# A two-layer encoder trunk on one core: the order of layer two's beginning left to the scheduler, and one operand sum moved from VectorE to an accumulating transfer

## The chip, the core and the metric

The kernel runs on one core of one Trainium2 chip. The metric is the device time of one execution in microseconds (us), as the median of several runs. The profile is one further execution, taken by the hardware profiler. Its engines are PE (TensorE; PEld is its weight load), DVE (VectorE), ACT (ScalarE), POOL (GpSimd) and SP (SyncE, which here only issues transfers). Each engine works through its own queue in order; engines wait for each other through semaphores.

## The reference

Two layers, each on the residual stream x of 512 rows by 2048 columns, all in float32:

```python
for l in range(DEPTH):                      # DEPTH = 2
    h = rmsnorm(x, pre_norm_g[l])
    z = h @ w_in[l]                         # 2048 -> 4928 columns
    q_lat, kv_lat, k_pe, gb, gc, xin, q_mem, gate = split_cols(z)
    ...                                     # latent attention, 8 heads: a_out
    c_out = short_gated_conv(gb, gc, xin, conv_w[l])
    mem_n = rmsnorm(mem, mem_norm_g[l])     # 256 memory tokens
    m_out = memory_attention(q_mem, mem_n, w_mk[l], w_mv[l])   # keys = mem_n @ w_mk, values = mem_n @ w_mv
    y = jnp.concatenate([a_out, c_out, m_out], axis=-1) * jax.nn.silu(gate)
    o = y @ w_o[l]                          # 2048 -> 2048
    x = x + rmsnorm(o, post_norm_g[l])
```

## The kernel before, in words

**Products in three matmuls.** Every float32 operand is split into a high piece (a rounded copy, made by ACT) and a low piece (operand minus high piece, made by DVE). A product is three matmuls: high by high, high by low, low by high (lines 296 to 298). For streamed weights the high piece is `wh` and the low piece `wl`: lines 212 and 216 for plain weights, lines 226 and 227 for the memory weights, which also take a gain. Three `wh` and three `wl` buffers rotate, so ACT can prepare a high piece once the matmuls three weight tiles back have ended.

**Seven block products.** The large products are cut into 2 by 2 blocks and done with seven block products P1 to P7 (a Strassen-Winograd scheme) whose operands are sums of blocks. Each block product runs over four steps c = 0 to 3; a step of 512 columns is 12 matmuls. The right-hand sums live in four raw tiles `T`, one for each c: T starts as block B11, becomes T1 for P5, T2 for P6 and T4 for P4. Sums are formed in two ways. `more` is a transfer on POOL's queue that adds a weight block into the tile as it arrives; it is issued once the low piece of the previous use is made. `plus` loads the block into a raw tile of its own, and DVE adds it (line 200); `other` adds a tile that is there already (line 202). Eight raw tiles rotate.

**The output projection** (`out_proj`) works on two pairs of 512-column blocks. The second pair uses the plan `FOUR`: passes P2, P1, then P3, P5, P6 and P7 interleaved by c, then P4. In it, `P5` adds block (0, 1), loaded by `plus`, to T and keeps the loaded tile under the name B12; `P6` adds the B22 tile to T; `P7` adds the kept B12 to B22.

**Side work.** What follows a block product (squares of the result for the post-norm, line 1205; the gain, line 1210; the residual sums `part`, line 1249) is put in a queue of deferred pieces. After each step the step's room is added to a budget (at most 2.5), and pieces are taken off while the budget covers their cost: 0.7 for a square and gain, 1.2 for half a residual row block.

**Layer two's beginning** comes right behind layer one's P4: 16 steps of memory keys and values (`mk` and `mv`, eight each, 24 and 12 matmuls), between them the transposes of the normalised rows, row block t = 0 to 3 in four banks each (call them T0 to T15; line 639 on PE). The normalisation of row block t is a Square over 2048 elements on ACT (`row_factor`, line 620), a power on POOL, and a scaled copy on ACT (`next_rows`, line 1277); the Square waits for both residual halves of that block. Then the input projection's first group starts with P1.

**What sets the order.** PE, SP and POOL always issue in the order in which the program was written. For DVE and ACT a scheduler chooses, except in written regions (`in_order(True)` to `in_order(False)`), where their instructions keep the written order among themselves. The scheduler still decides where instructions from outside a written region fall among those inside. In layer one the region runs from P1 of the last column pair, through layer two's memory steps and transposes, to the end of P1 and P2 of layer two's first group. In layer two it covers the last column pair alone.

Of the kernel before, what the change touches and what calls it, by code (L numbers as in the profile page):

```python
# [251 lines left out]
def encoder(tc, x, mem, positions, pre_norm_g, w_in, q_norm_g, w_uq, kv_norm_g, w_ukv, conv_w,  # L252
# [3 lines left out]
    nc = tc.nc  # L256
    depth = w_in.shape[0]
# [15 lines left out]
    add = pr.add  # L273
# [198 lines left out]
    def group(left, key, w, block, slot, passes, final, hold=None, by_two=False):  # L472
# [9 lines left out]
        def unit(q, c):  # L482
            def of(name, *loads, more=None, plus=None, alloc=None, **kw):
                return Unit((key, name, c), [block(h, j, c) for h, j in loads],
                            None if more is None else block(*more, c), None if plus is None else block(*plus, c), alloc,
                            **kw)
            if passes is FOUR and q in ("P5", "P6", "P7"):
                return {"P5": lambda: of("T", plus=(0, 1), keep=(key, "B12", c)),
                        "P6": lambda: of("T", other=(key, "B22", c)),
                        "P7": lambda: of("B22", other=(key, "B12", c))}[q]()  # L490
            if q == "P1":
                return of("P1" if apart else "T", (0, 0))
            if q == "P5":
                if passes is FIRST:
                    return of("T", (0, 0), more=(0, 1))
                return of("T", *([(0, 0)] if apart else []), plus=(0, 1))
            return {"P6": lambda: of("T", more=(1, 1)), "P4": lambda: of("T", more=(1, 0), alloc=hold),
                    "P2": lambda: of("P2", (1, 0)), "P3": lambda: of("B22", (1, 1)),
                    "P7": lambda: of("B22", plus=(0, 1))}[q]()
# [767 lines left out]
    def next_factor(t):  # L1267
        def f():
            pr.until(lambda: f"xo{t}" in G)
            xt, og = G[f"xo{t}"]  # L1270
            G[f"xr{t}"] = row_factor(xt, og)
        return f

    def next_rows(t):
        def f():
            xt, og = G.pop(f"xo{t}")
            nc.scalar.activation(og, xt, AF.Copy, scale=G[f"xr{t}"])
            G[f"hs{t}"] = og
        return f
# [52 lines left out]
    for l in range(depth):  # L1332
        G["left"] = L = Left(True)
        C, gs, owns = projection(l)

        def use(L=L):
            G["left"] = L
            G["ys"] = {}
        turn = [lambda l=l, t=t: transpose_rows(l, t, G[f"hs{t}"]) for t in range(NT)]
        if l == 0:  # L1340
            add(use)
            def turn_half(t, h, on=None):
                return lambda: transpose_rows(0, t, G[f"hs{t}"], (2 * h, 2 * h + 1), on)
            add(turn_half(0, 0))
            add(lambda: first_rows(1, (0,)))
            add(pr.begin_prep(1))
            add(lambda: left_half(0, (0,)))
            add(pr.begin_prep(2))
            add(turn_half(1, 0, nc.scalar))
            add(lambda: first_rows(1, (1,)))  # L1350
            add(lambda: left_half(1, (0,)))
            add(pr.begin_prep(3))
            add(lambda: first_factor(2))
            add(turn_half(0, 1))
        else:
            ms = mem_steps(l)
            put(ms[:1])
            for i in range(2):
                add(lambda i=i: mem_reload(2 + i))
            add(next_factor(0))  # L1360
            put(ms[1:2])
            add(next_rows(0))
            put(ms[2:3])
            add(use)
            side = {0: next_factor(1), 1: next_rows(1), 3: next_factor(2), 5: next_rows(2), 7: next_factor(3),
                    9: next_rows(3)}
            ms = [(f, u, 0.3 if k < 11 else 1.0) for k, (f, u, _) in enumerate(ms)]
            for n in range(16):
                t, q = n // 4, n % 4
                add(lambda t=t, q=q: transpose_rows(l, t, G[f"hs{t}"], (q,), nc.vector))  # L1370
                if t < 2 and q % 2:
                    add(lambda t=t, q=q: left_half(t, (q // 2,)))
                if t >= 2 and q == 3:
                    add(lambda t=t: right_half(t - 2))
                put(ms[n + 3:n + 4])
                if n in side:
                    add(side[n])
        (a, b), (a1, b1) = gs[0][:2], gs[1][:2]
        add(owns[0])
        if l == 0:  # L1380
            put(a[:1])
            add(first.close)
            add(turn_half(1, 1))
            add(lambda: left_half(0, (1,)))
            add(lambda: left_half(1, (1,)))
            add(lambda: first_rows(2))
            add(lambda: first_factor(3))
            add(lambda: first_rows(3))
            put(a[1:], b[:1])
            add(turn[2])  # L1390
            add(lambda: right_half(0))
            put(b[1:3])
            add(turn[3])
            add(lambda: right_half(1))
            put(b[3:])
        else:
            put(a, b)
            add(in_order(False))
        add(owns[1])
        put(a1, b1)  # L1400
        put(*gs[0][2:], *gs[1][2:])
        add(owns[2])
        put(gs[2][0])
        conv = [(conv_turn(l, c, C), []) for c in range(4)]
        put(weave(gs[2][1] + gs[2][2], conv, 2), *gs[2][3:])
        add(owns[3])
        put(*gs[3])
        add(owns[4])
        if l == 0:
            add(positions_load)  # L1410
        g4 = [s for steps in gs[4] for s in steps]
        put(g4[:4])
        add(lambda l=l, C=C: latents_begin(l, C))
        put(g4[4:8])
        if l > 0:
            add(lambda C=C: k_rope(C))
        put(g4[8:16])
        if l == 0:
            add(mem_load)
            G["mTd"] = dram.tile([4, P, D], F32, name="mTd")  # L1420
        lat = [latent_turn(l, "cq", j) for j in range(4)] + [latent_turn(l, "ckv", j) for j in range(2)] + [k_rope_turn] * (l > 0)
        gm = lambda t, C=C: C["gm"][:, t, :]
        more = [(f, []) for f in [gate_turn(12 + j, gm, j) for j in range(4)] + [qm_turn(j, C) for j in range(4)] + lat]
        if l == 0:
            more.insert(8, (mem_rows, []))
        put(weave(g4[16:], more[:11], 1))
        put(more[11:])
        gates = [gate_turn(j, lambda t, C=C, j=j: C["ga0" if j < 4 else "ga1"][:, t, :], j % 4) for j in range(8)]
        G["left"] = Y = Left(False)
        g0, g1, gains, fetch = out_proj(l)  # L1430

        def low(p):
            return lambda: G["left"].split("A12", p, G["ys"][2 + p][:, :, :256])

        def use_y(Y=Y):
            G["left"] = Y

        def sums(p):
            def f():
                a, b = G["ys"][p], G["ys"][2 + p]  # L1440
                left = G["left"]
                pr.defer(1.2, lambda: left.split("A11", p, a[:, :, :256]))
                pr.defer(1.2, lambda: left.split("A22", p, b[:, :, 256:]))
                combine(left, p, a[:, :, :256], b[:, :, :256], a[:, :, 256:], b[:, :, 256:])
            return f

        last_pair = {0: [(sums(0), []), g0[0][0]], 1: [g0[0][1]], 2: [g0[0][2]], 3: [g0[0][3]],
                     4: [g1[0][0]], 5: [g1[0][1]], 6: [g1[0][2]], 7: [g1[0][3]]}

        def route(l=l):  # L1450
            if l == depth - 1:
                G["src"], G["dst"] = G["dst"], out[0]
            else:
                G["src"], G["dst"] = x[0], dram.tile([S, D], F32, name="xs")
        add(route)
        mixer(l, C, gates, {6: [(use_y, []), (low(0), [])], 7: [(low(1), [])]}, last_pair)
        add(sums(1))
        add(gains(0))
        put(*g0[1:])
        add(gains(1))  # L1460
        four = {q: [g1[2][4 * c + k][1][0] for c in range(4)] for k, q in enumerate(("B22", "B12"))}
        for t, u in enumerate((g1[1][3][1][0], four["B22"][0], four["B22"][1], four["B12"][1])):
            u.behind = fetch(t)
        add(in_order(True))
        put(g1[1], g1[2][:14])
        if l + 1 < depth:
            for i in range(2):
                add(lambda i=i: mem_reload(i))
        put(g1[2][14:], g1[3])
        if l + 1 == depth:  # L1470
            add(pr.settle)
            add(in_order(False))
# [27 lines left out]
```

## Time and profile before

| | |
|---|---|
| runs, median of 3 | 1535.54 us (1534.11 to 1536.19) |
| the profiled execution, its own time | 1535.69 us |
| its span in the trace | 1533.9 us |
| mean granted TensorE clock | 0.994 |
| PE busy | 1494.0 us, 97% of the span |
| DVE busy | 1171.2 us |
| ACT busy | 861.9 us |

The span is what the trace covers; the profiled time lies 1.79 us above it. In a timeline row the first number is the start in us from the span's start, the second the duration; `[2.07 <-ACT wh L226]` at its end says how long the engine had been idle and what ended that. `x2` merges two instructions. In a row of stretches (windows) each engine has its busy time and its number of instructions; behind them stand the granted clock, the DMA engines' busy share and GB/s.

### The profile page before, as it was taken

How to read it: one execution, taken by the hardware profiler on the slowest of the kernel's cores; microseconds unless marked ns; L12 is line 12 of the kernel's file. 1: busy time of each engine (PE TensorE's matmuls, PEld its weight loads, DVE VectorE, ACT ScalarE, POOL GpSimd, SP SyncE). 2: the span in 40 equal slices, each digit the busy share in tenths (PEclk: the TensorE clock that was granted, in tenths of full speed). 3: DMA queues.
4: the chain of work that ended last, by engine and by line, in shares of the span. 5: the costliest groups of instructions: out<-in, count | busy, mean ns of one | idle time of the engine just before them, and what ended most of it. 6: DMA issues, size and time to landing. Idle time of an engine off the chain costs nothing.

```text
span 1533.9 us, 20277 instructions
## 1 busy us (share of the span) xinstructions
PE 1494.0 (97%) x7613; PEld 1278.0 (83%) x7613; DVE 1171.2 (76%) x1518; ACT 861.9 (56%) x1307; POOL 171.9 (11%) x189
## 2 busy tenths in 40 slices
PE   8999999999999999999998999999999999999995
PEld 7788888987898888888787888888988888888884
DVE  5987877675887668888778977887676776689787
ACT  8643534454667768645476543534454686775543
POOL 0212020221000000110210012020211000003001
PEclk9999999999999999999999999999999999999998
DMA  8989685979473112495776899695978421037743
GB/s 310 222 209 236 178 191 156 209 193 249 137 231 126 42 42 67 113 228 197 221 273 220 224 240 229 180 196 152 206 201 199 160 69 42 29 104 153 266 123 123
DMA packets 142030, 266.42 MB, mean 174 GB/s; under 512 B 17032, under 2 KB 39660, under 8 KB 138604
## 3 DMA queue, kind: packets, MB, share of 16 engines
q1 hardware_dynamic: 108904, 191.15, 38.8%
q0 software_dynamic: 32896, 73.93, 24.8%
q8 instruction: 59, 0.97, 0.3%
q14 instruction: 39, 0.32, 0.1%
q10 hardware_dynamic: 132, 0.05, 0.0%
HBM read 250.42 MB, written 14.68 MB: 173 GB/s over the span
## 4 chain that ended last, share of the span: by engine, by line
PE 76%; DVE 9%; ACT 6%; issue 6%; DMA 3%; POOL 1%; DVEq 0%; POOLq 0%; ACTq 0%; SPq 0%
PE P L297 18%; PE P L298 18%; PE P L296 18%; DMA wr<-in_w_in_dram 3%; DVE wl L216 2%; PE ptp L1064 2%; ACT wh L212 2%; PE tps L824 1%; PE o L297 1%; PE sc L296 1%; PE sc L297 1%; PE sc L298 1%; PE o L298 1%; PE o L296 1%; PE sc L1044 1%
## 5 line engine op out<-in xcount | busy, mean ns | idle before, releaser
L212 ACT CAST wh<-wr 128x1024 fp32r<-128x1024 f32 (+1 forms) x404 | 416.2, 1033 | 469.2 <-PE P L298 272.0
L216 DVE TENSOR_TENSOR wl<-wr,wh 128x1024 fp32r<-128x1024 f32 (+1 forms) x404 | 481.2, 1195 | 211.3 <-ACT wh L212 209.7
L296 PE MATMUL P<-wh,S 128*128 128x512 f32 (+1 forms) x896 | 346.7, 387 | 0.0
L297 PE MATMUL P<-wl,S 128*128 128x512 f32 (+1 forms) x896 | 345.1, 385 | 1.5 <-DVE wl L216 1.3
L298 PE MATMUL P<-wh,S 128*128 128x512 f32 (+1 forms) x896 | 344.1, 384 | 0.4 <-DVE S L434 0.4
L297 PE MATMUL P<-wl,A 128*128 128x512 f32 (+1 forms) x656 | 252.6, 385 | 7.1 <-DVE wl L216 7.1
L296 PE MATMUL P<-wh,A 128*128 128x512 f32 (+1 forms) x656 | 253.3, 386 | 0.5 <-ACT wh L212 0.5
L298 PE MATMUL P<-wh,A 128*128 128x512 f32 (+1 forms) x656 | 251.6, 384 | 0.5 <-DVE A L434 0.5
L297 PEld LDWEIGHTS P<-wl,S 128*128 128x128 f32 x896 | 168.6, 188 | 32.8 <-DVE wl L216 3.4
L298 PEld LDWEIGHTS P<-wh,S 128*128 128x128 f32 x896 | 168.6, 188 | 31.4 <-DVE S L434 0.9
L296 PEld LDWEIGHTS P<-wh,S 128*128 128x128 f32 x896 | 168.5, 188 | 29.7
L142 POOL DMA_DIRECT2D wr<-in_w_in_dram x84 | 101.7, 1211 | 555.3 <-DVE wl L216 400.1
L297 PEld LDWEIGHTS P<-wl,A 128*128 128x128 f32 x656 | 123.2, 188 | 30.9 <-DVE wl L216 9.4
L296 PEld LDWEIGHTS P<-wh,A 128*128 128x128 f32 x656 | 123.1, 188 | 23.4 <-ACT wh L212 1.6
L298 PEld LDWEIGHTS P<-wh,A 128*128 128x128 f32 x656 | 123.1, 188 | 23.2 <-DVE A L434 1.2
L200 DVE TENSOR_TENSOR wr<-wr,wr 128x1024 f32<-128x1024 f32 (+1 forms) x100 | 118.7, 1191 | 8.7 <-DMA wr<-in_w_in_dram 6.7
L1050 ACT ACTIVATE P<-sc,nm 128x512 f32<-128x512 f32 (+1 forms) x96 | 59.9, 625 | 36.7 <-DVE nm L1047 35.9
L1047 DVE TENSOR_REDUCE nm<-sc 128x1 f32<-128x512 f32 (+1 forms) x96 | 57.0, 596 | 12.2 <-PE sc L1045 6.7
L1053 ACT ACTIVATE P<-P,rec 128x512 f32<-128x512 f32 (+1 forms) x96 | 61.6, 658 | 6.0 <-DVE rec L1052 6.0
L302 DVE TENSOR_TENSOR PT<-ptp,PT 128x512 fp32r<-128x512 f32 (+1 forms) x96 | 56.2, 594 | 8.8 <-ACT PT L301 8.6
L226 ACT ACTIVATE wh<-wr,cols 128x512 fp32r<-128x512 f32 x64 | 43.6, 717 | 22.7 <-PE P L298 7.0
L227 DVE SCALAR_TENSOR_TENSOR wl<-wr,cols,wh 128x512 fp32r<-128x512 f32 x64 | 45.8, 747 | 13.4 <-ACT wh L226 13.4
(270 smaller groups left out, 2226.6 us busy)
## 6 DMA issues: line engine op xcount, KB each, us to landing
wr<-in_w_in_dram SPq DMA_DIRECT2D x172, 512.0 KB, 4.4
wr<-in_w_o_dram SPq DMA_DIRECT2D x72, 512.0 KB, 4.0
wr<-in_w_in_dram POOLq DMA_DIRECT2D x68, 512.0 KB, 7.1
wr<-in_w_in_dram SPq DMA_DIRECT2D x40, 416.0 KB, 3.8
wr<-in_w_o_dram POOLq DMA_DIRECT2D x24, 512.0 KB, 6.3
wr<-in_w_mk_dram SPq DMA_DIRECT2D x16, 512.0 KB, 4.7
wr<-in_w_mv_dram SPq DMA_DIRECT2D x16, 512.0 KB, 5.9
wr<-in_w_in_dram POOLq DMA_DIRECT2D x16, 416.0 KB, 5.8
```

The costliest lines, as they stand in the source:

```text
L142: engine.dma_start(dst, src, **kw)
L200: nc.vector.tensor_tensor(src, src, tiles[c], op=ALU.add)
L212: nc.scalar.copy(hi[:, :n], src)
L216: nc.vector.tensor_tensor(lo[:, :n], src, hi[:, :n].bitcast(F32), op=ALU.subtract)
L227: nc.vector.scalar_tensor_tensor(lo[:, h], src[:, h], g, hi[:, h].bitcast(F32), op0=ALU.mult, op1=ALU.subtract)
L296: nc.tensor.matmul(ps, ah, bh, start=first, stop=False, **kw)
L297: nc.tensor.matmul(ps, ah, bl, start=False, stop=False, **kw)
L298: nc.tensor.matmul(ps, al, bh, start=False, stop=last, **kw)
L302: nc.vector.tensor_tensor(lo, src, hi.bitcast(F32), op=ALU.subtract)
L1047: nc.vector.tensor_reduce(nmax, ps, axis=AX.X, op=ALU.max, negate=True)
L1050: nc.scalar.activation(pt, ps, AF.Exp, bias=nmax, accum_out=tot)
L1053: nc.scalar.activation(pt, pt, AF.Copy, scale=rec)
```

## The change

- **T1 by accumulating transfer.** In `FOUR`, P5's block (0, 1) is now added into T by a `more` transfer on POOL's queue, and P7 loads the same block again by `plus` and adds it on DVE. So in each layer four DVE additions (line 200) go, four transfers of 512 KB come. SP issues as many loads as before, in the same places of its queue. On POOL's queue the first two new transfers stand ahead of the two `gains` loads, which used to go first, the other two behind them. The four loads of residual rows (`fetch`) stay in place.
- **The written region of layer one ends at the end of P4**, not in layer two's first group. The memory steps, the transposes and the first passes are the scheduler's on DVE and ACT.
- **Less side work in layer one's P4**: each of its four steps adds 0.3 to the budget; before it was 1.4 for the first three and nothing for the last.
- **Memory steps of layer two** keep their room of 0.8, where it was 0.3 for most and 1.0 for the last ones.
- **Row blocks 2 and 3** are evicted from their transposes by ACT, in four pieces of 128 columns a bank with the gain as scale (line 645), no longer by DVE in one (line 641).
- **The Squares of row blocks 2 and 3** are written one transpose later.

```diff
             if passes is FOUR and q in ("P5", "P6", "P7"):
-                return {"P5": lambda: of("T", plus=(0, 1), keep=(key, "B12", c)),
-                        "P6": lambda: of("T", other=(key, "B22", c)),
-                        "P7": lambda: of("B22", other=(key, "B12", c))}[q]()
+                return {"P5": lambda: of("T", more=(0, 1)), "P6": lambda: of("T", other=(key, "B22", c)),
+                        "P7": lambda: of("B22", plus=(0, 1))}[q]()
...
-            side = {0: next_factor(1), 1: next_rows(1), 3: next_factor(2), 5: next_rows(2), 7: next_factor(3),
+            side = {0: next_factor(1), 1: next_rows(1), 4: next_factor(2), 5: next_rows(2), 8: next_factor(3),
                     9: next_rows(3)}
-            ms = [(f, u, 0.3 if k < 11 else 1.0) for k, (f, u, _) in enumerate(ms)]
             for n in range(16):
                 t, q = n // 4, n % 4
-                add(lambda t=t, q=q: transpose_rows(l, t, G[f"hs{t}"], (q,), nc.vector))
+                add(lambda t=t, q=q: transpose_rows(l, t, G[f"hs{t}"], (q,)))
...
             put(a, b)
-            add(in_order(False))
...
-        four = {q: [g1[2][4 * c + k][1][0] for c in range(4)] for k, q in enumerate(("B22", "B12"))}
+        four = {q: [g1[2][4 * c + k][1][0] for c in range(4)] for k, q in ((0, "B22"), (3, "B12"))}
...
-        put(g1[2][14:], g1[3])
+        put(g1[2][14:], [(f, u, 0.3) for f, u, *_ in g1[3]] if l + 1 < depth else g1[3])
+        if l + 1 < depth:
+            add(in_order(False))
```

The change takes away one line early in the file, so lines behind it are one lower in the rows of the changed kernel (1248 is 1249 of before, 619 is 620, 644 is 645). PE's and SP's queues hold the same rows in the same order. DVE's and ACT's differ at three places that matter below.

**DVE in layer one's P4.** `wl` with a `wr` of T is the low piece of a P4 step (`wl_6786` is step 1 of both kernels, then steps 2 and 3), `tot` the sum of a row block's squares, `xr` a residual half, and the two rows on a bank `P` finish P7. Before:

```order
L1242 TENSOR_REDUCE tot_646_6777<-ssqo_570_5630 128x1
L216 TENSOR_TENSOR wl_6786<-wr_6248,wh_6785 128x1024
L534 SCALAR_TENSOR_TENSOR og_5620<-P_639_6545,og_5620 128x512
L534 SCALAR_TENSOR_TENSOR og_5631<-P_640_6546,og_5631 128x512
L1249 SCALAR_TENSOR_TENSOR xr_6293<-og_5618,r_6773,xr_6293 128x1024 x2
L216 TENSOR_TENSOR wl_6808<-wr_6267,wh_6807 128x1024
L1249 SCALAR_TENSOR_TENSOR xr_6319<-og_5629,r_6781,xr_6319 128x1024
L216 TENSOR_TENSOR wl_6829<-wr_6291,wh_6828 128x1024
```

Changed:

```order
L1241 TENSOR_REDUCE tot_646_6777<-ssqo_570_5630 128x1
L1248 SCALAR_TENSOR_TENSOR xr_6293<-og_5618,r_6773,xr_6293 128x1024
L216 TENSOR_TENSOR wl_6786<-wr_6248,wh_6785 128x1024
L533 SCALAR_TENSOR_TENSOR og_5620<-P_639_6547,og_5620 128x512
L533 SCALAR_TENSOR_TENSOR og_5631<-P_640_6548,og_5631 128x512
L1248 SCALAR_TENSOR_TENSOR xr_6293<-og_5618,r_6773,xr_6293 128x1024
L1248 SCALAR_TENSOR_TENSOR xr_6319<-og_5629,r_6781,xr_6319 128x1024
L216 TENSOR_TENSOR wl_6808<-wr_6267,wh_6807 128x1024
L216 TENSOR_TENSOR wl_6827<-wr_6291,wh_6826 128x1024
```

A residual half now stands ahead of the low piece of step 1, and three in all ahead of that of step 2, where there were two. The scheduler has brought residual halves from outside the region into it.

**ACT where row block 2's Square falls.** The `wh` rows are high pieces of memory units; before, `wh_7121` is that of the fifth keys step (mk4) and `wh_7171` that of the fifth values step (mv4). Before:

```order
L226 ACTIVATE wh_7093<-wr_6869,cols 128x512 x2
L433 CAST A_673_7117<-hT_7010 128x1024
L226 ACTIVATE wh_7121<-wr_6891,cols 128x512 x2
L620 ACTIVATE og_5620,st_7156<-xr_6403 128x2048
L226 ACTIVATE wh_7171<-wr_6939,cols 128x512 x2
```

Changed, with `wh_7078` the high piece of mv3, `wh_7115` of mk4, `wh_7162` of mv4 and `wh_7201` of mk5:

```order
L226 ACTIVATE wh_7078<-wr_6863,cols 128x512 x2
L619 ACTIVATE og_5620,st_7184<-xr_6405 128x2048
L226 ACTIVATE wh_7115<-wr_6886,cols 128x512 x2
L1276 ACTIVATE og_5620<-xr_6405,r_7188 128x2048
L433 CAST A_670_7110<-hT_6989 128x1024
L226 ACTIVATE wh_7162<-wr_6934,cols 128x512 x2
L619 ACTIVATE og_5631,st_7333<-xr_6460 128x2048
L226 ACTIVATE wh_7201<-wr_6957,cols 128x512 x2
```

The Square of row block 2 stands one memory unit earlier, and that of row block 3 (`og_5631`) ahead of mk5, where before it stood ahead of mv6, three units later.

**ACT from transpose T11 on.** `hT` from `hps` is an eviction in four pieces, `Km` and `Vm` are the finished memory keys and values, `A` and `S` left-hand pieces, and `wh_7474` the high piece of P1's step 1; that of its step 2 comes three evictions of four pieces after the last row here. Changed:

```order
L644 ACTIVATE hT_7303<-hps_7410,cols 128x128 x4
L433 CAST A_692_7419<-hT_7303 128x1024
L301 CAST Km_7453<-mk_6894 128x256
L212 CAST wh_7474<-wr_7240 128x1024
L301 CAST Km_7453<-mk_6895 128x256
L644 ACTIVATE hT_7462<-hps_7463,cols 128x128
L301 CAST Km_7453<-mk_6894 128x256
L644 ACTIVATE hT_7462<-hps_7463,cols 128x128 x3
L301 CAST Vm_7490<-mv_6896 128x512
L433 CAST S_697_7499<-hT_7303 128x1024
L301 CAST Km_7453<-mk_6895 128x256
L301 CAST Vm_7490<-mv_6897 128x512
```

Before, the four-piece rows were single rows on DVE, and no ACT row stood for them.

## The prediction

> **What bounds the kernel now.** First the busy times on the page:
>
> ```profile
> PE 1494.0 (97%) x7613; PEld 1278.0 (83%) x7613; DVE 1171.2 (76%) x1518; ACT 861.9 (56%) x1307; POOL 171.9 (11%) x189
> ```
>
> TensorE has work for all but 40 us of the span, so a change that leaves its matmuls alone can only take away its waits. Then the waits of PE from 690 to 850 us, where nearly every edit falls (line, what it waited for, us in total, times, longest):
>
> ```profile
> PE P L297 <- DVE wl L216: 4.7, 5, 1.4
> PE mv L296 <- ACT wh L226: 2.7, 2, 2.1
> PE mk L298 <- DVE wl L227: 0.8, 1, 0.8
> PE mv L297 <- DVE wl L227: 0.6, 2, 0.3
> ```
>
> All are late weight pieces. The stretches of 10 us show where, and that the clock is lost too (PE busy is the first number, the granted clock the fraction behind POOL):
>
> ```profile
> 790.00:800.00 10.00, 9.10 (x59) 7.77 (x58) 7.38 (x9) 4.98 (x7) 1.89 (x4) 1.00 0.59 210
> 800.00:810.00 10.00, 9.20 (x57) 7.85 (x56) 7.17 (x11) 7.71 (x9) 0.00 (x0) 1.00 0.54 158
> 810.00:820.00 10.00, 7.60 (x39) 6.17 (x38) 7.67 (x11) 6.84 (x8) 1.89 (x4) 0.86 0.61 203
> 820.00:830.00 10.00, 9.08 (x61) 7.92 (x60) 7.80 (x12) 6.31 (x12) 0.59 (x1) 0.97 0.43 133
> 830.00:840.00 10.00, 8.87 (x38) 7.04 (x39) 10.00 (x12) 4.59 (x5) 0.54 (x1) 1.00 0.98 348
> ```
>
> PE lacks 0.90 + 0.80 + 2.40 + 0.92 + 1.13 = 6.15 us, and the clock 1.4 + 0.3 = 1.7 us.
>
> The whole loss of layer two's beginning comes from PE's timeline (start, duration, idle time before):
>
> ```profile
> 780.62 0.60 PE L639 MATMUL hps<-identr,og 128*128 128x128 f32 x4
> 793.67 0.60 PE L639 MATMUL hps<-identr,og 128*128 128x128 f32 x4
> 815.83 0.50 PE L296 MATMUL mv<-wh,mH 128*128 128x512 f32 x1 [2.07 <-ACT wh L226]
> 827.33 1.47 PE L639 MATMUL hps<-identr,og 128*128 128x128 f32 x12
> 834.08 0.50 PE L297 MATMUL P<-wl,A 128*128 128x512 f32 x1 [1.13 <-DVE wl L216]
> ```
>
> From transpose T1 (780.62) to T5 (793.67) PE does two rounds of one keys step, one values step and two transposes without a wait: 6.53 us a round. Six rounds from T1 give T13 at 819.8; it stands at 827.33. T13 to T15 take 1.2 us, P1's step 0 takes 2.73 (12 matmuls, 0.227 apart), and the second matmul of step 1 comes 0.23 after its first: 824.0 without a wait. It starts at 834.08. So **10.1 us** are lost here: 6.15 of idle PE, 1.7 of clock, and 2.2 that each restart costs beside its idle time, since a matmul after a wait takes 0.50 where others follow 0.227 apart.
>
> **Layer one's P4.** Here a fence shows DVE, POOL and PE together:
>
> ```profile
> 756.60 0.94 POOL L308 TENSOR_TENSOR r<-ms,mhalf 128x1 f32<-128x1 f32 x1
> 757.37 1.23 DVE L216 TENSOR_TENSOR wl<-wr,wh 128x1024 fp32r<-128x1024 f32 x1 [0.18 <-ACT wh L212]
> 758.51 1.28 DVE L534 SCALAR_TENSOR_TENSOR og<-P,og 128x512 f32<-128x512 f32 x2
> 758.65 0.50 PE L297 MATMUL P<-wl,A 128*128 128x512 f32 x1 [0.71 <-DVE wl L216]
> 759.71 2.47 DVE L1249 SCALAR_TENSOR_TENSOR xr<-og,r,xr 128x1024 f32<-128x1024 f32 x2
> 762.10 1.22 DVE L216 TENSOR_TENSOR wl<-wr,wh 128x1024 fp32r<-128x1024 f32 x1
> 763.37 0.50 PE L297 MATMUL P<-wl,A 128*128 128x512 f32 x1 [1.45 <-DVE wl L216]
> ```
>
> PE waits 0.71 for step 1's low piece and 1.45 for step 2's. In the changed queue a residual half comes ahead of step 1's piece. It needs `r`, ready at 757.54, so it runs from 757.6; by the pair at 759.71 one half takes 1.2. Step 1's piece then starts at 758.8, not 757.37, and PE goes on at 760.1. P7's two sums take 1.2 and the two other halves 2.4: step 2's piece starts at 763.5 and PE goes on at 764.8, not 763.37. Step 3's piece follows at once, before PE needs it at 767.5. **Cost: 1.4 us.** Less room for side work takes nothing off DVE's queue here, because the scheduler fills it. Bounds: 0.3, were gaps of DVE to take up most of it, to 2.4, two halves in full; the queue is known, so I take 1.4.
>
> **Layer two's beginning.** What made PE wait on ACT was this (DVE, then ACT):
>
> ```profile
> 793.01 2.48 DVE L1249 SCALAR_TENSOR_TENSOR xr<-og,r,xr 128x1024 f32<-128x1024 f32 x2
> 795.52 1.92 ACT L620 ACTIVATE og<-xr 128x2048 f32<-128x2048 f32 x1 [3.77 <-DVE xr L1249]
> 797.43 1.32 ACT L226 ACTIVATE wh<-wr,cols 128x512 fp32r<-128x512 f32 x2
> 813.16 1.91 ACT L620 ACTIVATE og<-xr 128x2048 f32<-128x2048 f32 x1 [3.76 <-DVE xr L1249]
> ```
>
> ACT stood 3.77 us at row block 2's Square, which needs two residual halves, while the next unit's high piece (797.43) was behind it; 3.76 at row block 3's. In the changed queues the halves stand earlier on DVE, and the Squares one and three memory units earlier, that is some 3.3 and 9.8 us, a round above being two units. PE's waits at these two places, 2.7 + 0.6 by the two `mv` rows of the waits, are covered by the smaller of them. With the 2.07 us wait the clock's drop behind it goes too.
>
> What comes instead is ACT's: eight evictions in four pieces. The groups, the last two being transfers with KB and us to landing:
>
> ```profile
> L645 ACT ACTIVATE hT<-hps,cols 128x128 f32<-128x128 f32 x40 | 10.7, 409 | 0.0
> L641 DVE TENSOR_TENSOR hT<-hps,cols 128x512 f32<-128x512 f32 x22 | 14.6, 684 | 0.9 <-PE hps L639 0.8
> L301 ACT CAST Km<-mk 128x256 fp32r<-128x256 f32 x4 | 1.4, 371 | 2.2 <-DVE Km L302 2.2
> L301 ACT CAST Vm<-mv 128x512 fp32r<-128x512 f32 x2 | 1.1, 588 | 0.0
> L212 ACT CAST wh<-wr 128x1024 fp32r<-128x1024 f32 x8 | 8.3, 1048 | 1.3 <-issue 1.3
> L200 DVE TENSOR_TENSOR wr<-wr,wr 128x1024 f32<-128x1024 f32 x84 | 102.3, 1223 | 7.8 <-DMA wr<-in_w_in_dram 6.2
> wr<-in_w_o_dram POOLq DMA_DIRECT2D x24, 512.0 KB, 6.3
> ```
>
> Four pieces take 4 x 10.7 / 40 = 1.07 us, eight evictions 8.6; DVE is freed of 8 x 0.684 = 5.5. ACT's busy time from 790 to 840 was 4.98 + 7.71 + 6.84 + 6.31 + 4.59 = 30.4; with 8.6 it is 39.0, in 50 - 10.1 = 39.9 us. That just fits. The tightest place is from T11's end to P1's step 2. ACT: T11 1.07, two casts of a high piece's size 2.1, four `Km` 1.5, two high pieces 2.1, T12 1.07, two `Vm` 1.2, T13 to T15 3.2 makes 12.2, then DVE's low piece 1.2: 13.4. PE: a round less one transpose, 6.1 (mk7, T12, mv7), T13 to T15 1.2, two P1 steps 5.5, and 0.2 to the first use of a low piece: 13.0. So PE waits 0.4 there, 0.6 with its restart. **Residue: 1.5 us**, this one and a few waits of its kind; bounds 0 (all fits) and 4.9 (below).
>
> **T1 by transfer.** Eight DVE additions of 1.223 go, 9.8 us off DVE; that none is on the path shows the next fence (DVE makes P1's step 0 piece, DVE adds for P5, ACT rounds P5's T, PE begins P5 and waits at P6):
>
> ```profile
> 695.50 1.23 DVE L216 TENSOR_TENSOR wl<-wr,wh 128x1024 fp32r<-128x1024 f32 x1 [0.55 <-ACT wh L212]
> 704.80 1.22 DVE L200 TENSOR_TENSOR wr<-wr,wr 128x1024 f32<-128x1024 f32 x1
> 708.01 1.06 ACT L212 CAST wh<-wr 128x1024 fp32r<-128x1024 f32 x1 [1.66 <-PE P L298]
> 713.25 0.39 PE L296 MATMUL P<-wh,S 128*128 128x512 f32 x1
> 716.82 0.50 PE L297 MATMUL P<-wl,S 128*128 128x512 f32 x1 [0.46 <-DVE wl L216]
> ```
>
> The sum is done at 706.0, but ACT can round it only at 708.01, when PE releases a buffer. The transfer may start at 696.7, when P1's low piece is made, and by the median of its kind lands 6.3 later, at 703.0. PE stands still only if it lands after 711.1 (713.48, the first use of P5's low piece, less 1.06 and 1.23), 14.4 us after its issue. The other three steps have longer. Behind the first two stand the gain loads on POOL, wanted after P1's end. The wait of 0.46 at P6 stays: P6's and P7's additions still stand ahead of its piece. So I cost this edit at **nothing** in both layers; SP's loads keep their number and places. P7's block has its raw tile for as long as before.
>
> **Sum.** 1535.69 (profiled) - 10.1 + 1.4 + 1.5 = 1528.5 us; the runs' median lies 0.15 below the profiled time: **1528.3 us**.
>
> [...]
>
> **The rivals.**
> - *The clock drops in P4.* PE's waits grow from 0.71 and 1.45 to about 2.1 and 1.8 within 7 us. For it: the 2.07. Against: 1.45 did nothing at 763, where the stretch kept 1.00. Price 1.7, as at 815: 1530.0.
> - *ACT becomes the bound.* 39.0 of 39.9 us leaves it no idle time. If it is busy only nine tenths of the time, the stretch lasts 39.0 / 0.9 = 43.3, 3.4 more: residue 4.9, 1531.7. For it: ACT's queue heads wait for PE's transposes. Against: one and three units of lead gained.
> - *P4 is relieved, as the change has it,* the scheduler's halves falling into idle time: neither the 1.4 nor the waits of 0.71 and 1.45: 1524.7. Against: an engine takes its queue in order.
> - *The change doesn't do what it says:* the waits move to other units, and 10.1 is lost as before: 1535 to 1537. Against: both Squares do stand elsewhere.
> - *Slower: the accumulating transfers land late.* P5's step 0 in each layer waits. It decides from 14.4 us after issue; to eat up the gain of 7.2 and 3.1 more, each layer has to lose 5.2, so a landing after 19.6: 1539 or more. Against: 6.3 median.
>
> **How the numbers follow.** Forecast 0.49, clock 0.20, ACT 0.16, P4 relieved 0.05, nothing gained 0.05, late transfers 0.05. A measurement here can tell 0.2%, 3.1 us: faster is under 1532.5, slower over 1538.6. Faster: 0.49 + 0.20 + 0.05 + two thirds of ACT's 0.16 = 0.85; slower 0.05; same 0.10. The range takes in residues of 0 to 4.9 and P4's cost down to 0.3: 1525.7 to 1532.3.
>
> **What would show it.** Right: between T1 and P1's step 2 PE loses under 2 us, no clock under 1.00 there, both Squares on ACT without idle time of over 1.5; PE's two waits for `wl` in P4 sum to 3 to 4.5; ACT's rounding of P5's T still ended by PE, not a transfer. Wrong: a wait on the `mv` or `mk` units over 1 us, a wait of P5 for its T, or a time over 1532.3.

## The result and the profile after

The changed kernel takes **1527.94 us** (median of 4, 1526.32 to 1528.30), the kernel before 1534.94 beside it: a ratio of **0.9949**, interval 0.9937 to 0.9961. Predicted were 1528.3 and a range of 1525.7 to 1532.3. The profiled execution took 1528.12 us, 7.57 less than the one of before.

The busy times on the page of the changed kernel:

```profile
PE 1490.4 (98%) x7613; PEld 1277.0 (84%) x7613; DVE 1157.1 (76%) x1502; ACT 868.8 (57%) x1339; POOL 186.6 (12%) x197
```

The waits of PE from 690 to 850 us:

```profile
PE P L297 <- DVE wl L216: 3.9, 4, 2.1
PE P L296 <- ACT wh L212: 0.5, 1, 0.5
```

All waits of the memory units (`mk`, `mv`) are gone; what is left belongs to weights of P steps. The stretches of 10 us, as in the prediction:

```profile
790.00:800.00 10.00, 10.00 (x71) 9.24 (x70) 9.28 (x13) 9.42 (x12) 3.23 (x6) 1.00 0.84 261
800.00:810.00 10.00, 10.00 (x69) 9.03 (x68) 8.20 (x11) 8.92 (x17) 0.00 (x0) 1.00 0.67 191
810.00:820.00 10.00, 10.00 (x69) 9.16 (x69) 5.34 (x7) 8.22 (x19) 0.00 (x0) 1.00 0.65 196
820.00:830.00 10.00, 9.60 (x49) 7.74 (x48) 9.98 (x13) 9.99 (x24) 1.14 (x2) 1.00 0.65 246
830.00:840.00 10.00, 10.00 (x46) 8.28 (x45) 9.65 (x9) 7.03 (x9) 0.00 (x0) 1.00 0.88 273
```

PE lacks 0.40 of the 50 us, where it lacked 6.15, and the clock is full. PE's timeline has these rows for the first keys step, T1, T13, P1's step 1 (second matmul), P1's step 2 and the last matmul:

```profile
770.42 0.28 PE L296 MATMUL mk<-mH,wh 128*128 128x256 f32 x1
782.11 0.60 PE L638 MATMUL hps<-identr,og 128*128 128x128 f32 x4
821.27 1.47 PE L638 MATMUL hps<-identr,og 128*128 128x128 f32 x12
825.58 0.39 PE L297 MATMUL P<-wl,A 128*128 128x512 f32 x1
828.86 0.50 PE L297 MATMUL P<-wl,A 128*128 128x512 f32 x1 [0.40 <-DVE wl L216]
1510.93 0.39 PE L298 MATMUL P<-T4h,A 128*128 128x512 f32 x1
```

and the kernel before has these for the first keys step and the last matmul, which is P4's:

```profile
768.74 0.28 PE L296 MATMUL mk<-mH,wh 128*128 128x256 f32 x1
1518.60 0.39 PE L298 MATMUL P<-T4h,A 128*128 128x512 f32 x1
```

Against the rows of before (starts of the same matmuls; each change is taken from the row above it on):

| PE's matmul | before | after | this stage's change |
|---|---|---|---|
| P6's that waits (716.82 before) | 716.82 | 717.17 | +0.35 |
| first keys step (mk0) | 768.74 | 770.42 | +1.33 |
| T1 | 780.62 | 782.11 | -0.19 |
| P1 step 1, second | 834.08 | 825.58 | -9.99 |
| the last | 1518.60 | 1510.93 | +0.83 |

The sum is -7.67. The gain and the loss each stand where the prediction put them: 9.99 us against a computed 10.1, and 1.33 against 1.4.

P4 of layer one, on DVE of the changed kernel:

```profile
757.86 1.28 DVE L1248 SCALAR_TENSOR_TENSOR xr<-og,r,xr 128x1024 f32<-128x1024 f32 x1 [0.39 <-POOL r L308]
759.06 1.22 DVE L216 TENSOR_TENSOR wl<-wr,wh 128x1024 fp32r<-128x1024 f32 x1
760.20 1.28 DVE L533 SCALAR_TENSOR_TENSOR og<-P,og 128x512 f32<-128x512 f32 x2
761.39 2.47 DVE L1248 SCALAR_TENSOR_TENSOR xr<-og,r,xr 128x1024 f32<-128x1024 f32 x2
763.79 2.35 DVE L216 TENSOR_TENSOR wl<-wr,wh 128x1024 fp32r<-128x1024 f32 x2
```

and on its PE:

```profile
760.33 0.50 PE L297 MATMUL P<-wl,A 128*128 128x512 f32 x1 [2.07 <-DVE wl L216]
763.60 0.49 PE L296 MATMUL P<-wh,A 128*128 128x512 f32 x1 [0.47 <-ACT wh L212]
765.06 0.50 PE L297 MATMUL P<-wl,A 128*128 128x512 f32 x1 [0.96 <-DVE wl L216]
```

The half ahead of step 1's low piece, DVE standing 0.39 us for `r` in front of it, and PE held 2.07 behind both: this is the queue that the prediction walked through. With the 0.35 us by which this run was late already, its 760.1 and 764.8 would be 760.45 and 765.15.

### The profile page after: what moved, and what is told of

Same layout as the page of the kernel before. It is cut to its first block, busy times and chain, and to the rows that moved or that the text cites. A ratio compares the mean times of both kernels' runs of the same rounds, so it can differ in the third digit from the quotient of the medians.

```text
span 1525.9 us, 20317 instructions
## 1 busy us (share of the span) xinstructions
PE 1490.4 (98%) x7613; PEld 1277.0 (84%) x7613; DVE 1157.1 (76%) x1502; ACT 868.8 (57%) x1339; POOL 186.6 (12%) x197
## 4 chain that ended last, share of the span: by engine, by line
PE 85%; DVE 6%; ACT 4%; issue 2%; DMA 1%; POOL 1%; DVEq 0%; POOLq 0%; SPq 0%; ACTq 0%
PE P L297 20%; PE P L298 20%; PE P L296 20%; PE ptp L1063 2%; DVE wl L216 2%; ACT wh L212 2%; PE tps L823 2%; PE o L297 1%; PE sc L296 1%; PE sc L297 1%; PE sc L298 1%; PE o L298 1%; PE o L296 1%; PE sc L1043 1%; PE sc L1044 1%
## 5 line engine op out<-in xcount | busy, mean ns | idle before, releaser
L142 POOL DMA_DIRECT2D wr<-in_w_o_dram x32 | 38.7, 1210 | 197.5 <-DVE wl L216 123.9
```

Of the source, the lines that this page charges most:

```text
L142: engine.dma_start(dst, src, **kw)
```

## The experiments

Each ratio is to runs of the kernel before made beside it; the medians come from several chips. A stage is given here as the time from P6's waited matmul (716.82 before) to T13, and from T13 to the last matmul; the two are free of what happens earlier in a run. Behind stand the half-clock periods in that profiled execution: at 377 us, in a stretch that no edit touches (below), and later. A half-clock period is priced at 1.7 us, by the one in the kernel before: its granted clock of 0.86 from 810 to 820 us and of 0.97 from 820 to 830 lacks 1.4 + 0.3 us.

| kernel | median us | ratio to before, interval | P6 to T13 | T13 to the last | half-clock at 377 / later |
|---|---|---|---|---|---|
| before | 1532.9 to 1539.0 (21 runs, one chip) | 1 | 110.51 | 691.27 | 1 / 1 |
| changed | 1527.94 | 0.9949, 0.9937 to 0.9961 | 104.10 | 689.66 | 1 / 0 |
| T1 alone | 1535.53 | 0.9997, 0.9988 to 1.0006 | 110.42 | 691.27 | 0 / 1 |
| region alone | 1525.60 | 0.9932, 0.9920 to 0.9945 | 103.77 | 689.13 | 0 / 0 |
| all but the region | 1539.25 | 1.0027, 1.0018 to 1.0036 | 110.06 | 695.95 | 0 / 3 |
| P4's rooms back | 1527.32 | 0.9943, 0.9931 to 0.9955 | 103.74 | 690.60 | 0 / 0 |
| evictions back | 1526.98 | 0.9946, 0.9934 to 0.9959 | 104.12 | 690.39 | 0 / 0 |
| both back | 1526.68 | 0.9937, 0.9924 to 0.9949 | 103.75 | 689.58 | 0 / 0 |
| late T1 | 1579.31 | 1.0283, 1.0267 to 1.0298 | 131.35 | 713.69 | 1 / 8 |
| P4 emptied, T0 later | 1528.85 | 0.9953, 0.9941 to 0.9966 | 104.47 | 691.79 | 0 / 1 |
| region alone, again | 1526.94 | 0.9939, 0.9926 to 0.9951 | 103.76 | 689.02 | 0 / 0 |
| changed, again | 1527.25 | 0.9940, 0.9927 to 0.9952 | 104.12 | 689.23 | 1 / 0 |
| region, T0 later | 1525.78 | 0.9935, 0.9923 to 0.9947 | 102.70 | 688.99 | 1 / 0 |
| region ahead of P4, T0 later | 1525.65 | 0.9931, 0.9918 to 0.9945 | 102.17 | 690.60 | 0 / 0 |

### T1 alone

The kernel before with the edit to P5 and P7 and nothing else.

```diff
-                return {"P5": lambda: of("T", plus=(0, 1), keep=(key, "B12", c)),
-                        "P6": lambda: of("T", other=(key, "B22", c)),
-                        "P7": lambda: of("B22", other=(key, "B12", c))}[q]()
+                return {"P5": lambda: of("T", more=(0, 1)), "P6": lambda: of("T", other=(key, "B22", c)),
+                        "P7": lambda: of("B22", plus=(0, 1))}[q]()
```

> The kernel before with the T1 edit alone (P5's block by accumulating transfer, P7's by load and addition). Theory A (the end of the written region carries the gain): within 1 us of the kernel before, about 1535, since none of the eight additions was on the path; PE's waits from 690 to 850 as before (4.7 on wl, 2.7 on the mv units' high pieces), and ACT's rounding of P5's T ended by PE. Theory B (9.8 us less on DVE carries it): 3 us faster or more.

0.9997, with both stages as before (110.42 and 691.27). Eight additions, 9.8 us of DVE's work, buy nothing. ACT's rounding of P5's T in this kernel:

```profile
705.49 1.05 ACT L212 CAST wh<-wr 128x1024 fp32r<-128x1024 f32 x1 [1.67 <-PE P L298]
```

It is ended by PE giving a buffer free, after 1.67 us, as before after 1.66; not by the transfer.

### The end of the region, alone and left out

First the kernel before with the region's end moved, and nothing else:

```diff
             put(a, b)
-            add(in_order(False))
...
         put(g1[2][14:], g1[3])
+        if l + 1 < depth:
+            add(in_order(False))
```

> The kernel before with one edit: the written region of layer one ends at the end of P4 and is not continued in layer two. P4's rooms, DVE's evictions, the additions and the memory steps' rooms are as before. Theory A: faster than the changed kernel, about 1525.8, since P4 loses 1.3 us less (no residual half ahead of step 1's low piece) and the wait of 0.4 to 0.6 at P1's step 2 goes with ACT's evictions. Theory B: about 1535; a mixed theory (order and DVE relief half each): 1531.

1525.60: the whole gain is in these two lines. PE in P4 and at T0, from its timeline:

```profile
757.24 0.50 PE L297 MATMUL P<-wl,A 128*128 128x512 f32 x1 [0.70 <-DVE wl L216]
760.50 0.50 PE L296 MATMUL P<-wh,A 128*128 128x512 f32 x1 [0.48 <-ACT wh L212]
761.96 0.50 PE L297 MATMUL P<-wl,A 128*128 128x512 f32 x1 [0.96 <-DVE wl L216]
776.42 0.66 PE L639 MATMUL hps<-identr,og 128*128 128x128 f32 x4 [0.46 <-ACT og L1277]
```

P4's first wait stays at 0.70. In exchange T0 waits 0.46 for ACT's scaled rows, which the changed kernel does not; P1's step 2 does not wait.

Then the reverse, the changed kernel with its region ended in layer two's first group, as before:

```diff
             put(a, b)
+            add(in_order(False))
...
-        if l + 1 < depth:
-            add(in_order(False))
```

> The changed kernel, but with the written region ended where it ended before (in layer two's first group): T1 by transfer, P4's small room, ACT's evictions and later Squares all kept. Theory A: no gain, 1535 to 1539, the waits of the mk and mv units back at over 4 us, perhaps worse than before since ACT has 8.6 us of evictions more in a fixed order. Theory B (less DVE work and less side work in P4 carry it): about 1528 to 1530.

1.0027, slower than before by 3.5 us. ACT and PE of this kernel:

```profile
798.37 1.91 ACT L619 ACTIVATE og<-xr 128x2048 f32<-128x2048 f32 x1 [4.52 <-DVE xr L1248]
801.98 0.39 PE L296 MATMUL mk<-mH,wh 128*128 128x256 f32 x1 [2.38 <-ACT wh L226]
827.54 0.50 PE L296 MATMUL P<-wh,A 128*128 128x512 f32 x1 [1.44 <-DVE Km L302]
829.86 0.80 PE L297 MATMUL P<-wl,A 128*128 128x512 f32 x1 [1.83 <-DVE wl L216]
```

ACT stands 4.52 us at row block 2's Square, more than the 3.77 of before, with the next keys step's high piece behind it. Its stages differ from before's by -0.45 and +4.68, and in these stages it has two half-clock periods more than before, 3.4 us. So the Squares "a step later" and the evictions on ACT do not mend the wait on ACT; the end of the region does. By the rows it does so through the order that the scheduler then gives the residual halves and the Squares, which no run tests by itself. Part of the 3.5 us may come from the smaller rooms in P4, which leave side work to DVE among the memory steps; that was not separated.

### P4's rooms as before

```diff
-        put(g1[2][14:], [(f, u, 0.3) for f, u, *_ in g1[3]] if l + 1 < depth else g1[3])
+        put(g1[2][14:], g1[3])
```

> The changed kernel with P4's rooms as before (1.4 for three steps). Theory A: the 1.3 us that P4 lost come back, 1526.6, PE's waits in P4 about 0.7 and 1.5 and no half ahead of step 1's low piece. Rival: less side work in P4 helped what follows (T0 or the first mv units now wait for their normalised rows), and the time is 1528 or more.

1527.32, 0.6 below the changed kernel, which is no more than the scatter of the runs. PE's rows:

```profile
758.05 0.50 PE L297 MATMUL P<-wl,A 128*128 128x512 f32 x1 [0.66 <-DVE wl L216]
777.25 0.66 PE L638 MATMUL hps<-identr,og 128*128 128x128 f32 x4 [0.46 <-ACT og L1276]
```

P4's wait of 2.07 shrinks to 0.66, and T0's wait of 0.46 comes back. From P6's waited matmul to the first keys step PE takes 51.85 us here, 51.92 before and 53.25 in the changed kernel. So the smaller rooms caused the loss in P4: with them the halves leave the written region, and the scheduler puts one ahead of step 1's low piece. It takes the region's end as well: with the rooms small and the region not ended (the kernel with all but the region) the same stretch takes 51.16, less than before. The smaller rooms also made the rows of layer two early enough for T0. From P6 to T13 the two cases differ by 0.36 (104.10 and 103.74).

### The evictions of row blocks 2 and 3

The changed kernel with these evictions on DVE in one piece, as before, and then with P4's rooms back as well:

```diff
-                add(lambda t=t, q=q: transpose_rows(l, t, G[f"hs{t}"], (q,)))
+                add(lambda t=t, q=q: transpose_rows(l, t, G[f"hs{t}"], (q,), nc.vector))
```

> The changed kernel (1527.94) with row blocks 2 and 3 evicted from their transposes by VectorE in one piece, as before. Theory A (ScalarE had just enough time; its evictions cost only the wait at P1's step 2, 0.40 us idle and 0.56 with its restart): 1527.4, and PE does not wait between 820 and 835 us. Theory B (ScalarE nearly bound holds up more than that one wait): 1526 or less. Theory C (VectorE, with 5.5 us more to do there, becomes the one that is late): 1529 or more, with new waits on low pieces between 790 and 835 us.

> The changed kernel with both P4's rooms and the evictions of row blocks 2 and 3 as before. What is left of the change is the end of the region, T1 by transfer, the memory steps' rooms and the Squares' places. Theory A (the two edits add up, P4's rooms 0.6 and the evictions 0.6): 1526.8, so some 1 us above the kernel with the region's end alone (1525.6) stays with the Squares, the rooms or T1. Theory B (these two edits are all that keeps the change from the region's end alone): 1525.6.

1526.98 and 1526.68. PE's waits from 690 to 850 us in the first:

```profile
PE P L297 <- DVE wl L216: 3.5, 3, 2.1
PE P L296 <- ACT wh L212: 0.5, 1, 0.5
```

Against the changed kernel one wait of 0.4 is gone, the one at P1's step 2, and no new one has come. By the waits that is theory A: ACT had time enough, and the evictions cost this one wait. The second median is near the 1526.8 of theory A, 1.1 above the region's end alone. Differences of this size, though, are no larger than the scatter of single runs (1526.04 to 1530.25 for the evictions alone), so the medians do not decide between the theories.

### T1's transfer written late

The kernel before with the T1 edit, and each P5 transfer written one unit ahead of its use. On POOL's queue it then stands behind the T4 transfer of the step before, which waits for P6's low piece:

```diff
+                if c + 1 < len(seq) and seq[c + 1].keep == "late":
+                    flush()
+                    more(c + 1)
...
-                        if c in after and seq[after[c]].more is not None:
+                        if c in after and seq[after[c]].more is not None and seq[after[c]].keep != "late":
```

> The kernel before with T1 by accumulating transfer, but the transfer written one unit ahead of its use, so that on POOL's queue it stands behind the transfer of T4 for the step before, which waits for P6's low piece. At step 0 nothing is lost; at each of steps 1 to 3 of both layers the transfer is issued some 5 us later than the tile is wanted less its landing. Theory A (the early issue is what hides the transfer): with landings of 6.3 to 9.8 us each of the six steps loses 1 to 4.4 us, so 1542 to 1562, and PE's waits in P5 end on the tile's transfer through ScalarE's rounding. Theory B (the edit is cheap because VectorE's additions are gone, whenever the transfer comes): 1535.5, as with the early issue.

1579.31: 43.8 us above T1 alone, 7.3 for each of the six steps, and above the expected range. POOL, ACT and PE at layer one's step 1:

```profile
717.10 2.43 POOL L142 DMA_DIRECT2D wr<-in_w_o_dram  x2 [18.78 <-DVE wl L219]
728.80 1.04 ACT L215 CAST wh<-wr 128x1024 fp32r<-128x1024 f32 x1 [11.17 <-DMA wr<-in_w_o_dram]
729.89 0.79 PE L299 MATMUL P<-wh,S 128*128 128x512 f32 x1 [4.92 <-ACT wh L215]
731.15 0.79 PE L300 MATMUL P<-wl,S 128*128 128x512 f32 x1 [0.47 <-DVE wl L219]
```

The second of the two transfers is issued at 717.85 and lands 10.9 us later, and ACT starts at 728.80; PE stands 4.92 us, and starts again at half clock (a matmul of 0.79 instead of 0.50). The mechanism was expected, the price was not: the landing is later than 9.8, and the clock comes on top. The granted clock of this run was 0.986, against 0.996 in the profiled one of T1 alone: it has nine half-clock periods against one, and the eight more make 8 x 1.7 = 13.6 us, an estimate by that price. So the T1 edit is free because of its place in POOL's queue, not by itself.

### Better orders

Three attempts on top of the region's end. The first empties the budget for side work at P6's last step and gives P4's steps none, and brings the transposes one memory unit later; the second has the later transposes alone; the third adds to these that the region ends ahead of P4.

```diff
+            if passes is FOUR and k == 2 and not hold:
+                steps[14] = (steps[14][0], steps[14][1], -2.5)
...
-            put(ms[2:3])
+            put(ms[2:4])
...
-                put(ms[n + 3:n + 4])
+                put(ms[n + 4:n + 5])
...
+        put(g1[2][14:], [(f, u, 0.0) for f, u, *_ in g1[3]] if l + 1 < depth else g1[3])
```

> The kernel before with the region's end moved behind layer one's P4 (1525.6), and beside it: in layer one the budget for side work is emptied at P6's last step and P4's steps add nothing to it, and layer two's transposes come one memory unit later. Theory A (P4's waits, 0.70 + 0.48 + 0.96 us idle, come from residual halves ahead of low pieces, and T0 waits for its rows only for want of one unit): both go, for 1.5 to 3 us: 1522.6 to 1524.1. Theory B (the halves put off make the rows of layer two late by more than the 2.7 us of one unit): 1526 to 1528, with T0 or T4 waiting.

1528.85, a miss, and neither theory's place. P4 has one wait, but of 2.12 us, and T0 waits still, a unit later (PE's timeline):

```profile
761.60 0.78 PE L297 MATMUL P<-wl,A 128*128 128x512 f32 x1 [2.12 <-DVE wl L216]
780.50 0.66 PE L641 MATMUL hps<-identr,og 128*128 128x128 f32 x4 [0.57 <-ACT og L1279]
```

The side work taken out of P6 and P4 comes on DVE at 756 us instead (P7's last sums, three gains, and behind them a residual half), again ahead of step 1's low piece. And behind this wait the clock drops: the waited matmul takes 0.78 us, not 0.50, and the granted clock from 762 to 766 us is 0.62.

```diff
-            put(ms[2:3])
+            put(ms[2:4])
...
-                put(ms[n + 3:n + 4])
+                put(ms[n + 4:n + 5])
```

> The region's end alone and the transposes one memory unit later. Theory A (T0 waits 0.48 us idle, 0.62 with its restart, for the scaled rows of block 0, and the keys step behind it 0.28, only because ScalarE makes the rows too late by less than a unit of 2.7 us): both go, 1524.7. Theory B (moved later, row blocks 2 and 3 come too late for P1, and a wait there takes the place of the one removed): 1525.6 or more, with waits between 815 and 835 us.

```diff
-        put(g1[2][14:], g1[3])
+        put(g1[2][14:])
+        if l + 1 < depth:
+            add(in_order(False))
+        put(g1[3])
```

> As the kernel before it, but the written region ends ahead of P4. In the queues the high pieces of steps 2 and 3 then stand ahead of ScalarE's copies, one residual half ahead of step 1's low piece and none ahead of step 2's. Theory A (waits follow the queues): step 1's wait grows from 0.70 to 2.07 us, as in the changed kernel (with its restart from 0.87 to 2.23), the two at step 2 (0.64 and 1.23 with restarts) go, so 0.5 us below the kernel before it, 1524.2. Theory B (a wait of 2.07 us costs a half-clock period, as at 815 us before): 1.7 us more than that, 1525.9.

1525.78 and 1525.65. Both do to PE's waits what theory A said, but their medians lie at theory B's figures (1525.6 and 1525.9) and not at A's 1524.7 and 1524.2. In the first T0 no longer waits, and P6 to T13 falls from 103.77 to 102.70. In the second PE has one wait in P4 and none at T0, and the stage is 102.17:

```profile
759.26 0.50 PE L297 MATMUL P<-wl,A 128*128 128x512 f32 x1 [2.10 <-DVE wl L216]
881.30 0.50 PE L297 MATMUL P<-wl,S 128*128 128x512 f32 x1 [0.76 <-DVE wl L216]
```

But in that execution 1.5 us are given back behind T13 (690.60 against 689.13), half of it in the second row, at a P step of layer two whose low piece waits for ACT's high piece. Waits of this kind come and go between executions of one kernel (0.39 us at 1135.75 in one of the two profiled executions of the changed kernel, none there in the other); their cause was not looked for. Neither median is measurably below the one of the region's end alone.

### The changed kernel and the region alone, side by side

> The kernel with the region's end alone once more, beside the changed kernel on one chip. Theory A (the rest of the change costs some 2 us: 0.6 at P1's step 2, 0.6 net in P4, the remainder by T1, the Squares and the memory steps' rooms): 1525.6, 2 us below the changed kernel of this call. Theory B (the difference of 2.3 us between the two earlier medians, 1525.6 and 1527.94, came from the chip or the moment): the two medians within 1 us of each other.

> The changed kernel once more, for the same comparison. Theory A: 1527.6 to 1528; theory B: within 1 us of the kernel with the region's end alone.

1526.94 and 1527.25 on one chip: within 1 us, so theory B by its own bound. With the earlier runs the medians are 1525.66 (10 runs) for the region's end alone and 1527.28 (9 runs) for the whole change, while the intervals of the ratios overlap. The stages put 0.35 us of a difference between P6 and T13, in both pairs of profiles, and 0.2 to 0.5 behind it. So the rest of the change is worth nothing or costs some 0.6 to 0.9 us by the profiles, 1.6 by these medians; which of these holds stays open. No kernel here measurably beats the changed one. Two moved lines do as well as all of it.

## Why the prediction was right

**The loss of layer two's beginning (-10.1).** Measured from T1 to P1's step 1: 53.46 us before and 43.47 now, 9.99. All parts of it went, the idle time, the restarts and the half-clock period. The prediction credited the move of both Squares by one and three memory units. DVE of the changed kernel has row block 2's last residual half, and ACT the two Squares, at

```profile
786.34 1.27 DVE L1248 SCALAR_TENSOR_TENSOR xr<-og,r,xr 128x1024 f32<-128x1024 f32 x1
787.65 1.92 ACT L619 ACTIVATE og<-xr 128x2048 f32<-128x2048 f32 x1 [0.77 <-DVE xr L1248]
795.55 1.91 ACT L619 ACTIVATE og<-xr 128x2048 f32<-128x2048 f32 x1
```

with 0.77 us of idle time and none, where it was 3.77 and 3.76. That it is the region's end which does this, and not the Squares' new places in the program, the diff did not tell apart and the two region runs did. The Squares account for 3.3 of the 6.15 us of idle time and for the clock. The prediction counted the other 2.85 (0.8 at a keys step, 0.92 and 1.13 at P1) as gone without saying by what. For P1 the rows show it: before, DVE starts the low pieces of its steps 0 and 1 at 828.69 and 832.82, behind finished keys, values and evictions in the written order; now it starts them at 816.02 and 821.42. With the region's end alone they are early as well (813.95 and 818.99).

**P4 (+1.4).** Measured 1.33. The sum of PE's idle time is 2.07 + 0.47 + 0.96 = 3.50; the two waits for `wl` alone make 3.03, at the lower end of the 3 to 4.5 named. One thing was not foreseen: step 2's first matmul waits 0.47 for ACT's high piece, since two copies of ACT, which wait for P7's sums on DVE, and a square between them stand ahead of it. It takes its time from the wait behind it, so the end came out right, in this by luck. The rival that P4 is relieved fell, and the run with the rooms back shows why: the smaller rooms are what lets the halves out of the region.

**The residue (+1.5).** This term was sized too large. The wait at P1's step 2 is 0.40, as computed (0.56 with its restart), and up to 850 us no other of its kind came. The last stage lost 0.83 in all, and 0.41 in the second profiled execution, which lacks a wait of 0.39 that this one has at 1135.75. ACT is busy for 9.42 + 8.92 + 8.22 + 9.99 = 36.6 of the 40 us from 790 to 830, so "just fits" held; the 39.0 computed was some 2 too high, since row block 2's Square, 1.92 us, now comes ahead of 790. The rival of ACT as the bound fell with the run that took the evictions off it and gained one wait.

**T1 at nothing.** Right, as T1 alone shows. The working behind it was too easy, though. In the changed kernel the first transfer is issued and its group lands so (the last row from the transfers issued from 690 to 720 us: KB, median us to landing):

```profile
697.49 1.21 POOL L142 DMA_DIRECT2D wr<-in_w_o_dram  x1 [33.00 <-DMA wr<-in_w_o_dram]
wr<-in_w_o_dram POOLq DMA_DIRECT2D x5, 512.0 KB, 9.8
```

9.8 us and not 6.3 (9.2 for the first transfer by itself), at a time when the DMA engines are busy for 0.99 of the stretch. So the tile is complete at 706.7, not 703.0, 1.7 us before ACT rounds it (708.37, ended by PE here too), and 4.7 before PE would stand (711.1 and the 0.35 of this run). The issue comes 0.40 behind the end of P1's low piece (697.09), as the prediction had it; the next transfer comes 0.40 behind its low piece as well (699.80, then 700.21). The row names a load as what ended the wait; the load of T's own block it can't be, since ACT had rounded T at 694.77. The bound that carried the term, 14.4 us after issue, held.

**The clock's drop in P4 as a rival.** It did not happen in the profile of the changed kernel, behind 2.07 us. The 2.07 at 815 was a weak argument for it, though: behind waits of 2.07 to 2.14 us the clock dropped in some executions and not in others (last section).

**The sum.** 1535.69 - 9.99 + 1.33 + 0.83 and the two small differences of +0.35 and -0.19 make 1528.0 by PE's stages, against 1528.12 in the profiled run. The forecast for the profiled run, 1528.5, was 0.4 too high: the residue was 0.7 too large, and this run came 0.35 late out of a part that the change does not touch (it is 0.34 late at the wait at 376 us already). That two errors of opposite sign nearly cancel is luck, and single runs of the changed kernel scatter by 2 us. One slip did not matter: the upper end of the range, 1532.3, does not follow from the residue of 4.9, which gives 1531.7.

## What to carry to other kernels

Work out a wait that is to go from the first to the last matmul that it delays, with the restarts and the clock, and not from the sum of idle times: 6.15 us of idle time were 10 us here. When a planner holds back side work, ask who places it then: smaller rooms put more of it ahead of the urgent piece. A transfer that replaced an engine's work was free here (a ratio of 0.9997) only from its place in its queue; the same transfer one unit before its use cost 7 us a step.

## What the runs showed of the hardware

**The length of PE's wait alone did not tell whether the clock dropped behind it.** Every profiled execution here has a wait of 2.13 or 2.14 us at about 376 us, in work that no edit touches, and behind it the clock dropped in 5 of the 14. In the changed kernel it is this row of PE's timeline:

```profile
376.68 0.66 PE L823 MATMUL tps<-identr,gm 128*128 128x128 f32 x4 [2.14 <-ACT y L834]
```

The changed kernel in stretches around it (PE's busy time first, the granted clock behind POOL):

```profile
374.00:377.00 3.00, 0.86 (x6) 0.44 (x5) 1.81 (x2) 1.91 (x3) 0.00 (x0) 1.00 1.05 434
377.00:381.00 4.00, 4.00 (x14) 3.22 (x12) 0.39 (x1) 0.71 (x2) 0.00 (x0) 0.57 1.02 413
```

and the kernel with the region's end alone, whose wait there is 2.13:

```profile
374.00:377.00 3.00, 0.87 (x7) 0.44 (x6) 1.81 (x2) 2.03 (x3) 0.00 (x0) 1.00 1.03 416
377.00:381.00 4.00, 4.00 (x22) 3.33 (x21) 0.27 (x1) 1.56 (x3) 0.00 (x0) 1.00 1.00 406
```

PE is as busy in the first stretch, 0.86 and 0.87 of 3 us, and in the second the clock is 0.57 in the one kernel and 1.00 in the other. Why it drops behind one of two such waits and not behind the other is not shown by these runs. At the price of 1.7 us, two runs of one kernel can differ by 1.7 us through the wait at 376 alone, an estimate; of the two profiled executions with the region's end alone neither lost the clock there, of the changed kernel's both did.

**P4's wait in the changed kernel may cost the clock in other runs.** It has 2.07 us of idle time, like the one at 815 before. In the profiled execution the clock stayed full behind it (the view of stretches again):

```profile
756.00:760.00 4.00, 2.27 (x10) 1.53 (x9) 3.43 (x6) 1.62 (x3) 3.12 (x4) 1.00 1.06 410
760.00:764.00 4.00, 3.19 (x12) 2.17 (x12) 4.00 (x6) 3.09 (x6) 1.65 (x3) 1.00 1.04 402
```

and the second one has 1.00 from 750 to 770 us as well. The kernel with P4 emptied, whose wait in P4 is 2.12, did lose the clock there:

```profile
755.00:762.00 7.00, 4.88 (x21) 3.79 (x20) 6.54 (x11) 5.64 (x12) 4.23 (x6) 0.97 1.05 404
762.00:766.00 4.00, 4.00 (x12) 3.14 (x12) 3.80 (x5) 0.00 (x0) 0.00 (x0) 0.62 1.09 429
```

The one with the region ended ahead of P4 has a wait of 2.10 in P4 and kept 1.00 from 750 to 770 us. So a loss of the clock in P4 of the changed kernel is possible in other runs; no profiled run shows it, nor how often it would come.
